# Second half of the projection columns exchanged between two passes: v beside k, retention's q and k beside q

## The chip, the core and the metric

The kernel runs on one core of a Trainium2 chip. The metric is device time in microseconds of one execution, as the median of several. The core's engines run side by side, each through its own queue in order, and meet by semaphores: TensorE (PE) multiplies, VectorE (DVE), ScalarE (ACT) and GpSimd (POOL) work elementwise, SyncE (SP) issues most transfers; ACT and POOL issue some from their own queues.

## The reference, cut

```python
h = rms_norm(x, norm_gain)                    # x: 4096 x 1024
proj = h @ w_in                               # 1024 x 3584
qa, ka, va, ga, qr, kr, vr, gr = split(proj, (512, 512, 512, 512, 256, 256, 512, 512))
# A: 8 heads of 64, rotary positions, three dilated windows, merged by their denominators
attn = dilated_attention(rope(qa), rope(ka), va)
# B: 4 heads, key 64, value 128, decay, in chunks of 128, GroupNorm
ret = group_norm(retention(rotate(qr), rotate(kr), vr)) * ret_gn_gain
mixed = concat([silu(ga) * attn, silu(gr) * ret])
out = rms_norm(x + mixed @ w_out, final_gain)
```

## The kernel before, in words

Three stages follow each other. Stage 1 projects x on q, k, v of the attention (`qa`, `ka`, `va`, here q, k, v) and on retention's `qr` and `kr` (here r), and stores them in DRAM, rotated and split into a high and a low part where attention needs it. Stage 2 runs attention over these and, as filler between its steps, retention in chunks c of 128 tokens, with `vr` projected chunk by chunk (weights `w2`, x chunks `hr`). Stage 3 does gates, output projection and the last norm.

Stage 1 makes two passes over the eight blocks of 512 tokens: blocks q = 0 to 7 are the first pass, 8 to 15 the second, `NBLK` is 8. A pass produces 512 output columns in two banks of PSUM: bank 0 is k in the first pass and q in the second; bank 1 is r in the first and v in the second. The product of a block is formed by seven smaller ones (Strassen and Winograd, `PRODUCTS` = P1 P5 P6 P3 P7 P2 P4) over halves of the columns, of the tokens (`half`) and of the 1024 inputs. Each is done in three matmul passes with high and low parts (`ops` in `product`). A product and a bank make one step, so a block is 14 steps (`STEPS`); block q begins at step s = 14 q. Which engine does what, and at which step, is written out by hand: `at(step, fn, ...)` puts a call into the list of a step; the loop at L773 issues the matmuls of a step and then its calls in the order of registration, which is by block. So each engine's queue follows steps, and within a step the older block comes first.

The calls of one block:

- `load_x` (POOL's queue) brings four quarters of x transposed; `sum_t` (DVE) makes the sums that the products need, `hi_x` (ACT) and `lo_x` (DVE, L316) split a product's input.
- `load_n` brings 128 rows of x into the one buffer `xn`; `square` (ACT, L330) sums their squares. After four of them `root` forms the scale (DVE, POOL: power at L337, `diag` at L339), `along_free` (PE, L348) spreads it along the row and `copy_rb` (ACT) stores it as `rb`. `rb` scales the tables of sines and cosines (`load_table` on POOL's queue, `scale_table` L369 on POOL); `rs` holds the scale by token, for v.
- `snapshot` (ACT, L418 or L416) copies a bank before the next product is added to it, `join` (DVE, L433 or L429) adds a snapshot to another bank. Bank 1 of the second pass is v: its snapshots and joins work on halves and multiply by the token's scale at once; `last_v` (DVE, L532) does the quarter without a snapshot. `store_values` writes v three times, by SP and by POOL.
- `rotate` (DVE, L477 to L482) turns a half of a bank by six instructions; `hi_o`, `lo_o` split q or k, `store_o` and `store_r` write them by SP.

`xn` and `diag` share one buffer (tag `xn`); v, r and the split q and k share four buffers (tag `hl`); seven buffers hold snapshots (tag `m`).

The weights of a pass are split ahead (`split_w`: ACT high, DVE or POOL low), those of the first in `start`, in the first steps; those of the second around step s = 112 (`load_raw`, `scale_b`, `diff_d`, `sum_s1` to `sum_s4`, `split`, `split_p4`), in space that the first pass gives free. Around step 224 `w2` is loaded and split (L83, L84), and the first chunks of x for retention are loaded and split (`split_h_chunk`, L816 to L819).

## Time and profile before

| | us |
|---|---|
| median of 3 runs | 2457.56 |
| lowest and highest | 2450.71, 2457.86 |
| profiled execution | 2460.55 |
| its span | 2458.7 |
| first product of stage 1 begins | 9.06 |
| first product of attention after its longest early wait | 831.01 |

The profile comes from one execution. A page gives busy time by engine, the span in 40 slices, the chain of work that ended last, and groups of instructions by source line; the trace behind it can be asked for any stretch, tile or line. In a row of groups stand line, engine, operation, output and input with their shapes, count, busy time in us and the mean of one in ns, then the idle time of the engine in front of them and what ended it. In a row of waits stand who waited, for whom, total us, times, and the longest. DVE is busy for 1757.4 us of the span, PE for 2306.5.

### The profile page before, as it was taken

What the parts mean: (1) busy time and instruction counts of PE and PEld (TensorE: products, weight loads), DVE (VectorE), ACT (ScalarE), POOL (GpSimd) and SP (SyncE); (2) the same over time, 40 slices, a digit from 0 to 9 for tenths busy, and PEclk for the clock granted to TensorE, in tenths of its full rate; (3) what the DMA queues carried; (4) which work ended last, traced back from release to release, by engine and by line L of the source; (5) the groups of instructions that cost most, each with busy time, mean ns of one, the idle gap of its engine ahead of it and who ended that gap; (6) DMA issues with size and microseconds to landing.
All of it is one profiled execution on the core that took longest, in us unless ns stands there. A gap on an engine that the chain in (4) does not pass through costs nothing.

```text
span 2458.7 us, 47420 instructions
## 1 busy us (share of the span) xinstructions
PE 2306.5 (94%) x16808; PEld 2072.8 (84%) x16808; DVE 1757.4 (71%) x4221; ACT 1115.2 (45%) x3036; POOL 903.1 (37%) x1053
## 2 busy tenths in 40 slices
PE   5798988699998799999999999998899999999998
PEld 5788988699998688888888888886789999999997
DVE  5778977977767587787877788786665565565554
ACT  3444433423333366666666666666322232232221
POOL 2444444344434454353534444446212112121110
PEclk8899999799999899999999999999999999999999
DMA  6454666366667858576585857655676665666663
GB/s 163 146 188 156 198 188 199 110 193 213 196 203 216 215 130 194 135 171 158 135 183 122 203 124 171 163 123 167 173 162 177 146 157 158 146 153 166 143 156 90
DMA packets 457597, 405.07 MB, mean 165 GB/s; under 512 B 207912, under 2 KB 411816, under 8 KB 452240
## 3 DMA queue, kind: packets, MB, share of 16 engines
q1 hardware_dynamic: 422496, 326.62, 52.3%
q0 software_dynamic: 34576, 75.16, 10.5%
q8 instruction: 133, 2.18, 0.4%
q14 instruction: 104, 0.85, 0.1%
q10 hardware_dynamic: 288, 0.26, 0.0%
HBM read 283.12 MB, written 118.64 MB: 163 GB/s over the span
## 4 chain that ended last, share of the span: by engine, by line
PE 68%; DMA 5%; DVE 5%; issue 2%; ACT 1%; SPq 1%; POOL 1%; POOLq 0%; DVEq 0%; ACTq 0%
PE S L1051 8%; PE x L397 7%; PE O L1121 7%; PE T L1088 5%; PE po L48 4%; PE po L50 4%; PE po L49 4%; PE g L50 4%; PE g L49 4%; PE g L48 4%; PE z L397 3%; PE V L48 2%; PE V L50 2%; PE V L49 2%; PE y L397 2%
## 5 line engine op out<-in xcount | busy, mean ns | idle before, releaser
L1072 DVE CUSTOM_DVE_ANT_0 S<-S,mask 128x256 f32<-128x256 f32 (+1 forms) x768 | 308.6, 402 | 165.7 <-PE S L1051 130.4
L1079 ACT ACTIVATE P<-S,nm 128x256 f32<-128x256 f32 (+1 forms) x768 | 337.2, 449 | 47.8 <-DVE nm L1072 44.8
L50 PE MATMUL g<-h,wg 128*128 128x256 f32 x1024 | 289.8, 283 | 0.0
L312 ACT ACTIVATE h<-xt 128x1024 fp32r<-128x1024 f32 (+1 forms) x115 | 119.2, 1037 | 236.1 <-DVE xt L304 107.1
L1635 POOL TENSOR_TENSOR rs<-v,mhalf 128x1 f32<-128x1 f32 x32 | 17.5, 547 | 549.0 <-DVE v L1633 493.5
L1088 PE MATMUL T<-ident,P 128*128 128x128 f32 x1368 | 213.2, 273 | 0.0
L49 PE MATMUL po<-wo,m 128*128 128x512 f32 x512 | 200.4, 391 | 0.0
L316 DVE TENSOR_TENSOR h<-xt,h 128x1024 fp32r<-128x1024 f32 (+1 forms) x115 | 150.8, 1316 | 64.9 <-ACT h L312 63.0
L50 PEld LDWEIGHTS g<-h,wg 128*128 128x128 f32 x1024 | 196.2, 192 | 0.0
L1121 PE MATMUL O<-pt,v 128*64 128x128 f32 (+1 forms) x1968 | 195.6, 325 | 0.0
L1051 PE MATMUL S<-kk,qc 128*128 128x256 f32 x1024 | 187.2, 306 | 7.4 <-issue 2.9
L48 PE MATMUL po<-wohi,m 128*128 128x512 f32 x448 | 178.7, 399 | 6.7 <-ACT m L40 5.6
L1051 PEld LDWEIGHTS S<-kk,qc 128*128 128x128 f32 x1024 | 149.7, 190 | 36.0 <-issue 17.8
L819 POOL TENSOR_TENSOR hc<-hr,hc 128x512 fp32r<-128x512 f32 x64 | 88.0, 1376 | 250.4 <-ACT hc L818 182.3
L50 PE MATMUL po<-wohi,m 128*128 128x512 f32 x448 | 176.7, 395 | 0.2 <-DVE m L41 0.2
L1121 PEld LDWEIGHTS O<-pt,v 128*64 128x64 f32 x1968 | 120.9, 136 | 60.5 <-issue 31.5
L1574 ACT ACTIVATE e<-g 128x256 f32<-128x256 f32 x128 | 48.2, 378 | 256.0 <-PE g L50 241.3
L1088 PEld LDWEIGHTS T<-ident,P 128*128 128x128 f32 x1368 | 163.7, 141 | 0.2 <-ACT wg0hi L87 0.2
L1079 ACT ACTIVATION_READ_ACCUMULATOR P<-S,nm 128x1 f32 x768 | 157.6, 205 | 0.0
L40 ACT ACTIVATE m<-e 128x256 fp32r<-128x256 f32 x128 | 53.1, 417 | 214.0 <-DVE e L1581 129.7
L49 PE MATMUL g<-h,wg1hi 128*128 128x256 f32 x512 | 146.6, 287 | 2.8 <-DVE h L867 2.5
L48 PE MATMUL g<-h,wg1hi 128*128 128x256 f32 x512 | 145.2, 285 | 4.1 <-ACT e L1574 3.4
(275 smaller groups left out, 6640.5 us busy)
## 6 DMA issues: line engine op xcount, KB each, us to landing
hr<-in_xT_dram SPq DMA_DIRECT2D x64, 512.0 KB
q<-dr_q SPq DMA_DIRECT2D x128, 256.0 KB
xt<-in_xT_dram POOLq DMA_DIRECT2D x60, 512.0 KB, 6.5
wb<-dr_w SPq DMA_DIRECT2D x128, 192.0 KB
o<-dr_o SPq DMA_DIRECT2D x192, 128.0 KB
v<-dr_v SPq DMA_DIRECT2D x94, 256.0 KB
xn<-in_x_dram POOLq DMA_DIRECT2D x32, 512.0 KB, 5.1
dr_k<-hl SPq DMA_DIRECT2D x64, 256.0 KB
```

The lines of the kernel that those rows point to most:

```text
L48: nc.tensor.matmul(out, wh, xh, start=first and i == 0, stop=False)
L49: nc.tensor.matmul(out, wh, xl, start=False, stop=False)
L50: nc.tensor.matmul(out, wl, xh, start=False, stop=last and i == n - 1)
L312: nc.scalar.activation(xs[q, prod][:, 0, ks, :], xq[(q, *SOURCE[prod])][:, ks, :], AF.Copy)
L316: (engine or nc.vector).tensor_tensor(h[:, 1, ks, :], src[:, ks, :], f32(h[:, 0, ks, :]), ALU.subtract)
L397: nc.tensor.matmul(o, l, r, start=first and j == 0, stop=last and j == 2, skip_group_check=True)
L819: nc.gpsimd.tensor_tensor(hc[:, :, 1, :], src, hc[:, :, 0, :].bitcast(F32), ALU.subtract)
L1051: nc.tensor.matmul(s[:, j * 256 : (j + 1) * 256], qq[h, t, half][:, off : off + 128] if br == 0 else it["q"][:, t, i, :], rhs, start=(j == ...
L1072: nc.vector.tensor_tensor_reduce(sv, sv, mask[:, it["br"], c0:256], 1.0, BIG, ALU.add, ALU.min, accum_out=nm[:, col : col + 1])
L1079: nc.scalar.activation(it["P", i // 2][:, i % 2, c0:256], sv, AF.Exp, bias=nm[:, col : col + 1], scale=-1.0, accum_out=den[:, col : col + 1])
L1088: nc.tensor.transpose(t[:, j * 128 : (j + 1) * 128], it["P", bank][:, j // 2, j % 2 * 128 : j % 2 * 128 + 128], ident)
L1121: nc.tensor.matmul(o[64 * bank : 64 * bank + 64, c0 : c0 + 128 * m], vt[h, br, idx // 8][:, idx % 8, :], it["pt"][:, a : a + m, :].rearran ...
```

## The change

The columns of bank 1 trade places: v is projected in the first pass, with k, and r in the second, with q. So `values` on ACT scales and copies v into its output tile after plain snapshots and joins, and R tables are loaded, scaled and used in the second pass. `load_n` goes to ACT's queue, the next one right after the square that frees the buffer; squares get new steps, and `along_free` comes two steps after `root` instead of one. All tables are scaled on DVE. At the passage to the second pass the raw weights come in row blocks by `load_w`, and `scale_b` and `sum_s1` one step later. In the last block the R rotation of half 1 and its store come earlier. `w2` is loaded two steps earlier and split three earlier (the first two row blocks; the others likewise), and the high parts of the first chunks, as well as their first two values, are ACT's.

```diff
-            nc.sync.dma_start(dst[:, 0:256].rearrange("k (u c) -> k u c", c=128), pairs_of(rows, 0 if ps else 512, part))
-            if ps == 0:
-                nc.sync.dma_start(dst[:, 256:512].rearrange("k (u c) -> k u c", c=128), pairs_of(rows, 1024, part))
+            halves = [h.rearrange("k (u c) -> k u c", c=128) for h in (dst[:, 0:256], dst[:, 256:512])]
+            nc.sync.dma_start(halves[0], pairs_of(rows, 0 if ps else 512, part))
+            if ps:
+                nc.sync.dma_start(halves[1], pairs_of(rows, 1024, part))
...
-            nc.gpsimd.dma_start(xn[q, i], io["x"][n * 128 : (n + 1) * 128, :])
+            nc.scalar.dma_start(xn[q, i], io["x"][n * 128 : (n + 1) * 128, :])
...
+            if i < 3:
+                load_n(q, i + 1)
...
-            nc.gpsimd.tensor_tensor(tabs[q, n, half], tabs[q, n, half], rb, ALU.mult)
+            nc.vector.tensor_tensor(tabs[q, n, half], tabs[q, n, half], rb, ALU.mult)
...
-                    if q >= NBLK and bank == 1:
+                    if q < NBLK and bank == 1:
...
-        def is_v(q, bank):
-            return q >= NBLK and bank == 1
-
-        def rcol(q, half, u):
-            n = 4 * (q % NBLK) + 2 * half + u
-            return rs[:, n : n + 1]
-
-        def snapshot(q, s, bank, name, half):
-
-            t = M[q, name, bank] = mp.tile([128, 512], F32, tag="m", name="m1")
-            p = banks[q, s, bank]
-            if is_v(q, bank):
+        def snapshot(q, s, bank, name):
+
+            M[q, name, bank] = mp.tile([128, 512], F32, tag="m", name="m1")
+            nc.scalar.activation(M[q, name, bank], banks[q, s, bank], AF.Copy)
+
+        def join(q, s, bank, name):
+
+            t = M[q, name, bank]
+            nc.vector.tensor_tensor(t, banks[q, s, bank], t, ALU.add)
+
+        vfs = {}
+
+        def values(q, half):
+
+            vf = vfs[q, half] = hlp.tile([128, 2, 512], F32, tag="hl", name="vo1")
+            parts = (M.pop((q, "u2", 1)), M.pop((q, "m5", 1))) if half else (M.pop((q, "m1", 1)), banks.pop((q, "x", 1)))
+            for i, p in enumerate(parts):
...
-                    us = slice(256 * u, 256 * u + 256)
-                    nc.scalar.activation(t[:, us], p[:, us], AF.Copy, scale=rcol(q, half, u))
-            else:
-                nc.scalar.activation(t, p, AF.Copy)
-
-        vfs = {}
-
-        def join(q, s, bank, name, half, part):
-
-            t, p = M[q, name, bank], banks[q, s, bank]
-            if is_v(q, bank):
-                vf = value_tile(q, half)
-                for u in range(2):
-                    us = slice(256 * u, 256 * u + 256)
-                    nc.vector.scalar_tensor_tensor(
-                        vf[:, u, 256 * part : 256 * part + 256], p[:, us], rcol(q, half, u), t[:, us], ALU.mult, ALU.add
+                    n = 4 * q + 2 * half + u
+                    nc.scalar.activation(
+                        vf[:, u, 256 * i : 256 * i + 256], p[:, 256 * u : 256 * u + 256], AF.Copy, scale=rs[:, n : n + 1]
...
-            else:
-                nc.vector.tensor_tensor(t, p, t, ALU.add)
-
-        def value_tile(q, half):
-            if (q, half) not in vfs:
-                vfs[q, half] = hlp.tile([128, 2, 512], F32, tag="hl", name="vo1")
-            return vfs[q, half]
...
-        def last_v(q):
-
-            vf, p = value_tile(q, 0), banks[q, "x", 1]
-            for u in range(2):
-                nc.vector.tensor_scalar(vf[:, u, 256:512], p[:, 256 * u : 256 * u + 256], rcol(q, 0, u), None, ALU.mult)
-
...
-                a, d = {1: (-3, 2), 2: (-7, 2), 3: (-10, 2), 4: (-14, 3)}.get(q, (-16, 3))
+                a, n = (-4 - 2 * (q - 1), (2, 4, 7, 9)) if q < 6 else (-14, (2, 5, 7, 10)) if q == 6 else (-15, (2, 5, 8, 11))
+                at(s + a, load_n, q, 0)
...
-                    at(s + a + d * i, load_n, q, i)
-                    at(s + a + d * i + d - 1, square, q, i)
-                e = s + a + 4 * d
-                at(e, root, q)
-                at(e + 1, along_free, q)
-                at(e + 1, copy_rb, q)
+                    at(s + a + n[i], square, q, i)
+                at(s + a + n[3] + 1, root, q)
+                late = a + n[3] + 3
+                at(s + late, along_free, q)
+                at(s + late, copy_rb, q)
...
-                if one or n == "A":
+                if n == "A" or not one:
...
-                    at(s + max(c, {0: 10, 1: 8}.get(q, 0)), scale_table, q, n, half)
+                    at(s + max(c, 10 if q == 0 else late + 1 if one else 0), scale_table, q, n, half)
...
+                at(s + 11, values, q, 1)
+                at(s + 12, store_values, q, 1)
+                at(s + 14, values, q, 0)
+                at(s + 15, store_values, q, 0)
+            else:
+                end = q == NB2 - 1
...
-                at(s + 17, rotate, q, 1, 1)
+                at(s + (11 if end else 17), rotate, q, 1, 1)
...
-                at(s + 18, store_r, q, 1)
-            else:
-                at(s + 11, store_values, q, 1)
-                at(s + 14, last_v, q)
-                at(s + 15, store_values, q, 0)
+                at(s + (14 if end else 18), store_r, q, 1)
...
-            raw[name] = t = ROOM[room](F32)
+            raw[name] = ROOM[room](F32)
...
-                rows = io["w1"][(k0 + k) * 128 : (k0 + k + 1) * 128, :]
-                nc.sync.dma_start(t[k][:, 0:256].rearrange("k (u c) -> k u c", c=128), pairs_of(rows, 0, part))
-            rows = by_blocks(io["w1"])[:, k0 : k0 + 4, 1536 + 256 * part : 1792 + 256 * part]
-            if room in ("wh0", "wh1", "p40"):
-                nc.sync.dma_start(WHOLE[room][:, :, 256:512], rows)
-            else:
-                for j, w in enumerate(WHOLE[room]):
-                    nc.sync.dma_start(w[:, :, 256:512], rows[:, 2 * j : 2 * j + 2])
+                load_w(1, raw[name][k], part, k0 + k)
...
-        at(s - 7, lambda: scale_b(raw["Bb"]))
...
-        at(s - 6, sum_s1)
+        at(s - 6, lambda: scale_b(raw["Bb"]))
+        at(s - 5, sum_s1)
...
-            ahead["hch"] = {0: [split_h_chunk(nc, hcp, raw["hr"], 0, j, nc.vector) for j in range(2)]}
+            ahead["hch"] = {0: [split_h_chunk(nc, hcp, raw["hr"], 0, j) for j in range(2)]}
...
-        at(s - 8, w2_load)
+        at(s - 10, w2_load)
...
-            at(s - 8 + i, w2_some, (2 * i, 2 * i + 1))
+            at(s - (10, 9, 8, 7)[i], w2_some, (2 * i, 2 * i + 1))
+            at(s - 6 + i, w2_split, (2 * i, 2 * i + 1))
...
-        for i in range(4):
-            at(s - 3 + i, w2_split, (2 * i, 2 * i + 1))
...
-        load_n(0, 0)
-        for n, half in (("A", 1), ("A", 0), ("R", 0), ("R", 1)):
-            load_table(0, n, half)
+        for half in (1, 0):
+            load_table(0, "A", half)
...
-        def squares(i):
-            square(0, i)
-            if i < 3:
-                load_n(0, i + 1)
-
...
-            4: lambda: (plus_times(Bb, Ab, 1, Bb, ALU.add), split_w(0, "P3", Bb)),
-            5: lambda: (squares(0), split_w(0, "P7", Aa, 0)),
-            6: lambda: (squares(1), split_w(0, "P2", Ab, 1)),
-            7: lambda: (squares(2), [load_w(0, Bb2[k], 1, 4 + k) for k in range(4)]),
-            8: lambda: squares(3),
-            9: lambda: (root(0), split_w(0, "P4", Bb2, 1)),
+            4: lambda: (load_n(0, 0), plus_times(Bb, Ab, 1, Bb, ALU.add), split_w(0, "P3", Bb)),
+            5: lambda: split_w(0, "P7", Aa, 0),
+            6: lambda: (square(0, 0), split_w(0, "P2", Ab, 1)),
+            7: lambda: ([load_w(0, Bb2[k], 1, 4 + k) for k in range(4)], square(0, 1)),
+            8: lambda: (square(0, 2), split_w(0, "P4", Bb2, 1)),
+            9: lambda: (square(0, 3), root(0)),
...
-                        if c < 2:
-                            nc.vector.tensor_scalar(res[c]["vch"], pv, ahead["rs"][:, c : c + 1], None, ALU.mult)
-                        else:
-                            nc.scalar.activation(res[c]["vch"], pv, AF.Copy, scale=ahead["rs"][:, c : c + 1])
+                        nc.scalar.activation(res[c]["vch"], pv, AF.Copy, scale=ahead["rs"][:, c : c + 1])
...
-                        hch[c].append(split_h_chunk(nc, hcp, hraw.pop(c), c, 1, nc.vector if c < 2 else None))
+                        hch[c].append(split_h_chunk(nc, hcp, hraw.pop(c), c, 1))
...
-                        hch[c + 1] = [split_h_chunk(nc, hcp, hraw[c + 1], c + 1, 0, nc.vector if c < 1 else None)]
+                        hch[c + 1] = [split_h_chunk(nc, hcp, hraw[c + 1], c + 1, 0)]
```

Left out of this diff: the table `WHOLE` of raw tiles, which only `load_raw` used, and the shorter argument lists of `snapshot` and `join`.

More of the change, by code (lines that the diff above doesn't have):

```diff
@@ L175, in phase1 @@
         make_identity(nc, ident)
-        WHOLE = {}
         def whole(p, tag):
             def get(dt):
-                t = WHOLE[tag] = p.tile([128, 4, 512], dt, tag=tag, name=f"w1{tag}")
+                t = p.tile([128, 4, 512], dt, tag=tag, name=f"w1{tag}")
                 return [t[:, k, :] for k in range(4)]
@@ L187, in get @@
             def get(dt):
-                ts = WHOLE["h0"] = [p.tile([128, n, 512], dt, tag=tag, name=f"w1{tag}") for tag in tags]
+                ts = [p.tile([128, n, 512], dt, tag=tag, name=f"w1{tag}") for tag in tags]
                 return [ts[k // n][:, k % n, :] for k in range(4)]
@@ L580, in phase1 @@
             for n, half, a, c in (("A", 1, -1, 3), ("A", 0, 2, 6), ("R", 0, 4, 8), ("R", 1, 6, 10)):
-                if one or n == "A":
+                if n == "A" or not one:
                     if q:
                         at(s + a, load_table, q, n, half)
-                    at(s + max(c, {0: 10, 1: 8}.get(q, 0)), scale_table, q, n, half)
+                    at(s + max(c, 10 if q == 0 else late + 1 if one else 0), scale_table, q, n, half)
             for bank in range(2):
                 if q:
-                    at(s + 1 + 2 * bank, snapshot, q, "x", bank, "m1", 0)
-                    at(s + 5, snapshot, q, "z", bank, "m5", 1)
-                at(s + 6 + bank, snapshot, q, "x", bank, "u2", 1)
-                at(s + 7 + bank, join, q, "z", bank, "u2", 1, 0)
-                at(s + 9 + bank, join, q, "x", bank, "m5", 1, 1)
-                at(s + 11 + bank, join, q, "y", bank, "m1", 0, 0)
+                    at(s + 1 + 2 * bank, snapshot, q, "x", bank, "m1")
+                    at(s + 5, snapshot, q, "z", bank, "m5")
+                at(s + 6 + bank, snapshot, q, "x", bank, "u2")
+                at(s + 7 + bank, join, q, "z", bank, "u2")
+                at(s + 9 + bank, join, q, "x", bank, "m5")
+                at(s + 11 + bank, join, q, "y", bank, "m1")
             at(s + 10, rotate, q, 0, 1)
@@ L738, in phase1 @@
         for bank in range(2):
-            snapshot(0, "x", bank, "m1", 0)
+            snapshot(0, "x", bank, "m1")
         sum_t(0, 1)
@@ L750, in phase1 @@
         for bank in range(2):
-            snapshot(0, "z", bank, "m5", 1)
+            snapshot(0, "z", bank, "m5")
         sum_t(0, 2)
```

## The prediction

> **What bounds the kernel now.** I read the page first (where in the span TensorE, PE, is not full), then a table of stages, then the waits inside the stages that are not full.
>
> ```profile
> span 2458.7 us, 47420 instructions
> PE   5798988699998799999999999998899999999998
> ```
>
> The second line is PE's busy share in 40 slices of 61 us: the holes are in slices 1 to 8 and around 13 and 28. The change touches the first 13 slices (the projection stage) and the beginning of the next stage. So the table is cut there: q0, q1 to q7 (rest of the first pass), q8 (the passage to the second pass), q9 to q15, and the passage to attention. Columns: length, busy time of PE, weight load, DVE, ACT, POOL with counts, granted clock, DMA share, GB/s.
>
> ```profile
> 0.00:90.65 90.65, 58.48 (x338) 53.28 (x339) 53.17 (x68) 39.09 (x61) 26.98 (x33) 0.85 0.57 145
> 90.65:435.68 345.03, 306.91 (x2369) 298.35 (x2367) 279.29 (x329) 140.89 (x194) 156.94 (x159) 0.95 0.59 182
> 435.68:507.74 72.06, 48.91 (x339) 48.13 (x338) 68.14 (x83) 29.13 (x43) 26.50 (x29) 0.81 0.41 124
> 507.74:788.20 280.46, 280.46 (x2354) 280.42 (x2352) 199.64 (x260) 95.54 (x146) 122.95 (x189) 1.00 0.70 213
> 788.20:831.01 42.81, 21.95 (x75) 15.67 (x73) 21.18 (x45) 2.75 (x8) 21.01 (x26) 0.72 0.81 222
> ```
>
> q9 to q15 are seven blocks in 280.46 us, PE busy in all of it: 40.07 us is what a block costs when PE sets the pace, 2.86 us a step. q1 to q7 hold the same number of products and take 345.03 us, 49.3 us a block: 64.5 us too much, of which 38.1 us is PE idle and 26.4 us is matmuls at a lower granted clock (0.95). An idle microsecond thus costs another 0.7 us. q8 takes 32 us too much, and the passage at 788.20 leaves PE idle for 20.9 us. What the change can win lies in these three rows; q9 to q15 can only lose.
>
> What PE waited for, first in q1 to q7, then in q8 (total, times, longest):
>
> ```profile
> PE rb L348 <- POOL diag L339: 14.7, 6, 4.2
> PE x L397 <- ACT m L418: 8.4, 4, 3.2
> PE z L397 <- ACT m L418: 5.0, 1, 5.0
> PE x L397 <- DVE m L433: 4.7, 1, 4.7
> PE x L397 <- DVE h L316: 3.0, 4, 1.2
> PE x L397 <- DVE o L478: 2.3, 1, 2.3
> ...
> PE x L397 <- DVE h L316: 11.9, 2, 8.0
> PE x L397 <- ACT m L418: 6.0, 1, 6.0
> PE x L397 <- DVE o L478: 5.2, 1, 5.2
> ```
>
> Two thirds of the 38.1 us are two things behind the sums of squares: the PE matmul that spreads the root over the row (`along_free`, waits for POOL's `diag`, 14.7 us) and snapshots that ACT makes late (13.4 us). Why ACT is late is in its own waits from q1 to q7:
>
> ```profile
> ACT xn L330 <- DMA xn<-in_x_dram: 98.7, 23, 8.8
> ACT rb L352 <- PE rb L348: 34.1, 7, 6.1
> ACT w1hr L277 <- DMA w1hr<-in_w_dram: 14.6, 1, 14.6
> ```
>
> ACT is busy for only 140.89 us of 345.03, but it stands for 98.7 us in front of squares whose rows are not there, with the snapshots queued behind it.
>
> **The change part by part.**
>
> *Who does what afterwards.* The rotations of retention leave the first pass and come into the second; v goes the other way. Prices, from q1 to q7 (first two rows and POOL's table row) and from q9 to q15 (the rest):
>
> ```profile
> L316 DVE TENSOR_TENSOR h<-xt,h 128x1024 fp32r<-128x1024 f32 x49 | 70.0, 1442 | 22.3 <-ACT h L312 22.2
> L369 POOL TENSOR_TENSOR tab<-tab,rb 128x512 f32<-128x512 f32 x28 | 52.2, 1867 | 0.4
> ...
> L316 DVE TENSOR_TENSOR h<-xt,h 128x1024 fp32r<-128x1024 f32 x48 | 60.9, 1268 | 36.0 <-ACT h L312 34.4
> L480 DVE TENSOR_TENSOR m<-m,tab 128x512 f32<-128x512 f32 x14 | 9.7, 692 | 0.5
> L429 DVE SCALAR_TENSOR_TENSOR vo<-z,rs_all,m 128x256 f32<-128x256 f32 x14 | 6.1, 480 | 15.1 <-PE z L397 15.1
> L416 ACT ACTIVATE m<-x,rs_all 128x256 f32<-128x256 f32 x28 | 11.6, 470 | 0.0
> ...
> 777.72 0.68 DVE L477 TENSOR_TENSOR t<-m,tab 128x512 f32<-128x512 f32 x1
> ...
> 781.46 0.68 DVE L433 TENSOR_TENSOR m<-y,m 128x512 f32<-128x512 f32 x1
> ...
> L454 POOL DMA_DIRECT2D dr_v<-vo x128 | 69.9, 553 | 108.4 <-DVE vo L429 70.3 <-DVE vo L532 38.1
> ```
>
> The last two timeline rows bracket one rotation: six instructions, 3.74 us. DVE in the first pass is busy 279.29/7 = 39.9 us a block, nearly the 40.07 that PE needs. It loses two rotations (7.5) and gains two scaled tables (2 x 0.69, by the broadcast product of L480). It also loses most of the stretching beside POOL's table products: `lo_x` takes 1442 ns here and 1268 where POOL does half as many, 1.2 us over seven. Estimate 39.9 - 7.5 + 1.4 - 1.2 = 32.6 us, 81%. ACT: 20.1 us + 8 value copies at 0.47 + four issues = 25.3 us a block.
>
> In the second pass DVE has 199.64/7 = 28.5 us. It loses eight half instructions of v (six L429, two of `last_v`: 8 x 0.48 = 3.8), gains three joins and four tables (7 x 0.69 = 4.8) and two rotations (7.5), and loses about 1 us of stretching: 36.0 us of 40.07, 90%. POOL is eased in both (16 issues of `dr_v` at 0.553 move forward; four row loads, two R tables and all products leave the first pass). SP's eight stores a block are dr_v for dr_r.
>
> *Squares.* The row load moves from POOL's queue, where it stood behind `load_x` and tables, to ACT right behind the square that frees the buffer.
>
> ```profile
> DMA to landing us min/median/max: 3.5/5.1/9.2
> ...
> L1547 ACTq DMA_DIRECT2D rt<-dr_ret x2: 351/356/362, 1709.8 to 1710.3; - x2
> ```
>
> A row lands 5.1 us after its issue, an issue on ACT's queue costs 0.36 us, and squares now stand two or three steps apart (5.7 or 8.6 us). So a wait of 98.7/23 = 4.3 us should fall to 0 or 1; behind the waiting square stand snapshots and `hi_x`. The matmul of `along_free` comes two steps after `root` instead of one: 2.86 us more against stalls of 14.7/6 = 2.5 us. What is late next: the DMA engines. The second pass is 0.70 x 40.07 = 28 us of DMA a block with v in it; the first takes that mix over and keeps four row loads (2.1 MB, 6.9 us at 213/0.70 = 304 GB/s), so 35 us, some 0.8 of a block (estimate). That is no bound, but rows will land later than 5.1 us at times, and `hi_o` gets its buffer only when v's stores are down. From both sides: if all three sources go, 64.5 us shrinks to nearly 4 (-60); if only DVE's part (10.0 of 38.1 us) goes, -17. I take a block of 43.3 us, nearer to the full effect because every named source is addressed: **-42 us**.
>
> *Start (q0).* The window before 44 us is full of DMA, and one row load and two R tables leave it, but the squares of q0 begin later.
>
> ```profile
> 10.00:44.20 34.20, 19.68 (x95) 17.83 (x95) 16.08 (x19) 13.02 (x21) 6.52 (x5) 0.88 0.99 227
> ...
> 58.81 1.04 ACT L330 ACTIVATE xn<-xn 128x1024 f32<-128x1024 f32 x1
> ...
> 74.62 1.06 ACT L330 ACTIVATE xn<-xn 128x1024 f32<-128x1024 f32 x1 [3.91 <-DMA xn<-in_x_dram]
> ...
> 78.28 1.13 PE L348 MATMUL rb<-diag,ones 128*128 128x512 f32 x2 [1.37 <-POOL diag L339]
> ```
>
> 1 MB at 227 GB/s is 4.6 us earlier for the weights. Four squares ran from 58.81 to 75.7. Now the first comes a step later, each next needs 1.06 + 0.36 + 5.1 = 6.5 us, and P4's split stands between the last two: the last ends near 79 and `along_free` near 81.5 instead of 78.28, with PE waiting 8 to 10 us for it while everything else is some 5 us ahead. Bounds -5 (weights only) and +8 (lost clock too); I take **+4 us**.
>
> *Passage to the second pass (q8).* DVE is busy 68.14 of 72.06 us: DVE sets this stage, with P1 to P4 of new weights to split. Out go q7's two rotations (7.5), in come four tables (2.8). Before it, ACT stood 14.6 us for raw weights behind retention's stores on SP's queue, and those stores are gone from there; the factor (`scale_b`) and the sum behind it come one step later. Against this the raw loads are 32 DMAs instead of 21 and their R half is in 512-byte pieces. DVE then needs some 61 us for 40 of PE, part of it paid out in q7, which ends with slack. Bounds -8 and -28, taken between: **-19 us**.
>
> *Second pass.* DVE's 36.0 us are unevenly laid. I add them up by step, with 0.62 us for a 512 form (3.74/6, the pitch inside the rotation) and 1.15 for a 1024 form (a little under twice, estimated). Steps 10 to 13 and 0 to 2 hold 5.0 (join, rotation, table), 2.9, 0.6, 5.0 (`lo_o`, rotation), 2.3, 4.9 (rotation, sum) and 1.15 us. Against 2.86 us a step, DVE is late by 2.1, 2.2, 0, 2.1, 1.6, 3.6 and 1.9 us after them. Step 3 then has a rotation (3.74), a sum and `lo_x` of P3 (2.3): done 8.0 us after the step's start, where PE needs it at step 6, after 8.6. By step 8 the lag is gone. So the bound is just met; nearest is the row of q9 to q15, which has no idle at all. Bounds 0 and +52 (eight blocks at 46.6 us, a third better than 49.3). I take half a microsecond a block: **+4 us**.
>
> *Passage to attention.* The last v is no longer stored there; the last R rotation of half 1 is drawn forward six steps, the split of w2 three or more, and the first chunks go to ACT.
>
> ```profile
> PE V L48 <- DVE hc L816: 4.8, 1, 4.8
> PE V L49 <- DVE w L84: 2.9, 1, 2.9
> ...
> 809.40 0.58 SPq L447 DMA_DIRECT2D dr_v<-vo  x1
> ...
> 814.01 4.10 SPq L523 DMA_DIRECT2D dr_q<-hl  x4
> ...
> 818.75 0.37 SPq L807 DMA_DIRECT2D hr<-in_xT_dram  x1
> ...
> 829.52 0.63 ACT L818 ACTIVATE hc<-hr 128x512 fp32r<-128x512 f32 x1 [24.83 <-DMA hr<-in_xT_dram]
> ```
>
> The 4.8 and 2.9 us go. `hr` of chunk 2 stands on SP behind four dr_v stores (4.6 us) and the last dr_q; now behind four dr_r and dr_q, released by a DVE that has no w2 splits left. Between -2 (only the wait for hc is saved) and -16 I take half of PE's idle 20.9: **-10 us**.
>
> **Sum:** +4 - 42 - 19 + 4 - 10 = -63 us, against this execution's own 2460.55 us (span 2458.7 and 1.9 around it). The median of the runs is 2457.56, 3 less, so the forecast is 2394 us.
>
> **The skill against the trace.** The row is the 98.7 us of waiting for xn. The Trainium skill, DMA: Bandwidth & Descriptors, "Issuing engines are not separate DMA queues", says that the engine which starts a DMA matters only for the sequencer's own time, since all run on the same 16 engines. By that rule alone the move to ACT's queue saves nothing of the transfer. The trace agrees that the transfer is not what is late (5.1 us against spacings of 5.7): my gain is in the order of issue.
>
> The row for tables on POOL is 1867 ns against DVE's 692. The Trainium skill, Perfetto Trace Analysis, "Optimizing Scalar/DVE Operations", advises the other direction where DVE is saturated, with a warning that the two engines share a read port. By it the second pass would keep four tables off DVE, 33.2 instead of 36.0 us a block, and its +4 in the sum would be 0 (2390 us in all); but `lo_x` at 1442 beside more of POOL's products and 1268 beside fewer shows that POOL's products stretch DVE's, so I keep the +4.
>
> **Rivals.**
> *Rows still late.* The squares' wait stays, because rows queue with v's stores. Then 28.1 us of the idle (diag, snapshots) and 0.7 of it in clock stay, 47.5 of 64.5: -17 instead of -42, 2419 us. For it: DMA at 0.8; against: 5.7 us of room. 18%. This is also what the Trainium skill, DMA: Bandwidth & Descriptors, would leave of the move by that sentence.
> *Everything goes.* First pass at -58, q8 at -27, tail -15, start -1, second pass +4: 2361 us. For it: PE without idle at 71% DVE in q9 to q15. 15%.
> *DVE saturates the second pass.* At 46.6 us a block +52 instead of +4: 2442 us. 7%.
> *The same, slower than before.* `lo_x` of P3 or P6 misses its step in every block and the lower clock doubles it, as in the first pass, where DVE at 81% kept PE waiting. From 48.4 us a block (63 + 4 over eight) the whole gain is gone. At a third of what q8 loses, 10.7 us a block, it is +85: 2475 us. Against it: no xn waits there, and POOL's products are gone. 6%. Another 4% ends between, without a measurable change.
>
> **How the numbers follow.** The forecast has 50% and alone spans 2375 to 2412. With the better case and late rows, 83%, the range is 2360 to 2430. 0.3% (7 us) is what a measurement here can tell. Faster: 50 + 18 + 15 + 7 = 90%; same 4%; slower 6%.
>
> **What would show it.** After: q1 to q7 near 303 us with ACT's wait for xn under 30 us and `along_free` under 5; q8 near 53; q9 to q15 within 286, DVE near 252 busy; first attention products 10 us closer to the end of the products; q0 a few microseconds longer with one wait of 8 us for diag. The forecast is wrong if PE shows waits for `lo_x` in every block of the second pass, or if ACT waits for buffers under v's stores.

## The result, and the profile after

| | before | after |
|---|---|---|
| median, us | 2456.43 (6 runs) | 2441.73 (6 runs) |
| lowest, highest | 2450.46, 2458.25 | 2438.32, 2446.74 |
| ratio after/before | | 0.9946, 95% interval 0.9929 to 0.9963 |
| profiled execution, its span | 2460.55, 2458.7 | 2446.74, 2445.0 |

Faster, but by 14.7 us (0.5%, the interval is clear of 1) and not by 63: 2441.73 lies outside the range 2360 to 2430. The page of the kernel after, PE's busy share in 40 slices of 61 us:

```profile
span 2445.0 us, 47407 instructions
PE   6789997899996899999999999998899999999998
```

The hole in slices 7 and 8 (the end of the first pass and the passage to the second) is shallower than before, that in slices 13 and 14 (the passage to attention) is still there, and slices 2 and 3, in the first pass, are still not full. The same stages of the kernel after (length, busy PE, weight load, DVE, ACT, POOL, granted clock, DMA share, GB/s):

```profile
0.00:89.15 89.15, 57.26 (x339) 51.18 (x339) 56.79 (x77) 44.97 (x70) 22.31 (x30) 0.81 0.56 157
89.15:421.19 332.04, 296.76 (x2369) 290.74 (x2367) 211.81 (x254) 162.02 (x244) 126.83 (x179) 0.95 0.70 219
421.19:482.65 61.46, 46.75 (x338) 45.63 (x337) 57.70 (x72) 29.97 (x44) 30.05 (x38) 0.86 0.57 169
482.65:768.80 286.15, 284.02 (x2354) 283.65 (x2352) 251.31 (x341) 90.76 (x125) 64.91 (x93) 0.99 0.56 170
768.80:818.78 49.98, 22.43 (x73) 16.22 (x73) 24.52 (x46) 5.67 (x14) 13.79 (x16) 0.71 0.70 171
```

| stage | before | after | difference | forecast |
|---|---|---|---|---|
| q0 | 90.65 | 89.15 | -1.5 | +4 |
| q1 to q7 | 345.03 | 332.04 | -13.0 | -42 |
| q8 | 72.06 | 61.46 | -10.6 | -19 |
| q9 to q15 | 280.46 | 286.15 | +5.7 | +4 |
| to the end of attention's early waits | 42.81 | 49.98 | +7.2 | -10 |
| rest | 1627.69 | 1626.22 | -1.5 | 0 |

DVE did what was worked out for it: 211.81/7 = 30.3 us a block in the first pass (32.6 forecast), 251.31 us in the second (252). DMA is at 0.70 in q1 to q7 where it was 0.59, and the clock there is 0.95 as before, with PE still idle for 35.3 us (38.1 before). What PE waited for in q1 to q7 of the kernel after (total, times, longest):

```profile
PE x L398 <- ACT m L406: 22.6, 5, 10.3
PE x L398 <- DVE m L411: 6.4, 1, 6.4
PE z L398 <- ACT m L406: 3.4, 3, 1.6
PE rb L349 <- POOL diag L340: 2.9, 3, 1.8
```

`along_free` fell from 14.7 to 2.9 us, DVE's many small waits are gone, and snapshots rose from 13.4 to 26.0. ACT's waits in the same stretch:

```profile
ACT xn L329 <- DMA xn<-in_x_dram: 73.0, 17, 8.8
ACT w1hr L276 <- DMA w1hr<-in_w_dram: 11.8, 2, 11.5
```

ACT still stands 73.0 us (98.7 before) in front of a square whose row has not landed. One such row, in ACT's timeline:

```profile
97.76 0.33 ACTq L322 DMA_DIRECT2D xn<-in_x_dram  x1
...
109.56 1.06 ACT L329 ACTIVATE xn<-xn 128x1024 f32<-128x1024 f32 x1 [6.80 <-DMA xn<-in_x_dram]
...
111.12 0.60 ACT L406 ACTIVATE m<-x 128x512 f32<-128x512 f32 x1 [0.41 <-ACT xn L329]
```

The row was asked for at 97.76, right behind the square that freed the buffer, and is squared at 109.56: 11.8 us later for a load whose median was 5.1 in the kernel before. The snapshot stands behind it, and PE behind the snapshot for 8.2 us. The stretch in which it was under way:

```profile
97.80:110.00 12.20, 5.77 (x49) 5.56 (x47) 5.65 (x5) 5.06 (x6) 2.56 (x4) 0.87 0.90 272
```

DMA share 0.90 at 272 GB/s: v's stores, which the first pass took over, run at this moment, beside k's stores and loads of tables and x.

### The profile page after: what moved, and what is told of

Read it like the earlier page. It is cut to its first block, busy times and chain, and to the rows that moved or that the text cites. A ratio compares the mean times of both kernels' runs of the same rounds, so it can differ in the third digit from the quotient of the medians.

```text
span 2445.0 us, 47407 instructions
## 1 busy us (share of the span) xinstructions
PE 2298.1 (94%) x16808; PEld 2065.6 (84%) x16808; DVE 1734.5 (71%) x4223; ACT 1141.5 (47%) x3082; POOL 803.8 (33%) x973
## 4 chain that ended last, share of the span: by engine, by line
PE 71%; DMA 11%; DVE 7%; issue 5%; ACT 3%; POOL 2%; SPq 1%; ACTq 0%; DVEq 0%; POOLq 0%
PE S L1019 8%; PE x L398 8%; PE O L1089 7%; PE T L1056 5%; PE po L48 4%; PE po L50 4%; PE po L49 4%; PE g L50 4%; PE g L48 4%; PE g L49 4%; PE z L398 4%; DMA xn<-in_x_dram 3%; PE V L48 3%; PE V L50 2%; PE V L49 2%
## 5 line engine op out<-in xcount | busy, mean ns | idle before, releaser
L315 DVE TENSOR_TENSOR h<-xt,h 128x1024 fp32r<-128x1024 f32 (+1 forms) x115 | 137.5, 1196 | 66.5 <-ACT h L311 66.4
L48 PE MATMUL g<-h,wg0hi 128*128 128x256 f32 x512 | 144.5, 282 | 1.7 <-ACT e L1539 1.7
```

The source lines that it names most:

```text
L48: nc.tensor.matmul(out, wh, xh, start=first and i == 0, stop=False)
L315: (engine or nc.vector).tensor_tensor(h[:, 1, ks, :], src[:, ks, :], f32(h[:, 0, ks, :]), ALU.subtract)
```

## The experiments

All start from the kernel after, unless another is named. Each time is a median with its ratio to the kernel before, run beside it on the same chip. The kernel before took 2456.43 to 2461.86 us there (medians), so the medians of two runs are comparable to some 5 us only, and where that matters the ratio decides. A view shows one execution: q1 to q7 took 332.04 us in the kernel after, and 330.94 and 324.62 in two runs below that change nothing in this stage (first chunks on DVE, q's loads on ACT). A few microseconds in one stage therefore say little.

**Only the squares.** The kernel before, with the change's loads and steps of the squares (row loads on ACT's queue behind the square, new steps, `along_free` two steps after `root`) and nothing else.

> The kernel before, with only the squares' part of the change: rows from ACT's queue behind the square, the new steps, along_free two steps after root; v stays in the second pass, tables on POOL. Theory: without v's stores in the first pass rows land in about 5 us, ACT's wait for xn falls from 98.7 to under 50 us and PE's for diag from 14.7 to under 6; q1 to q7 from 345 to 320 to 330 and the whole to 2432 to 2444, near the whole change's own 2441.7 or under it. Rival (ACT's queue is slow by itself): wait near 73 or over, the whole 2450 or over.

2447.05 us, ratio 0.9947 (0.9927 to 0.9966). In its q1 to q7, 331.9 us long, ACT waited:

```profile
ACT xn L330 <- DMA xn<-in_x_dram: 70.2, 20, 7.4
```

and among PE's waits there were:

```profile
PE x L399 <- DVE m L435: 6.9, 1, 6.9
PE x L399 <- DVE h L316: 6.5, 6, 1.3
...
PE z L399 <- ACT m L420: 3.8, 1, 3.8
```

The whole came a little above the range that was written down, and the wait for rows is well above the 50 expected. This part alone has the whole change's ratio (0.9946), so in the sum nothing can be told apart that the rest, exchange of columns included, brought. It is not that the rest did nothing: q8 is 70.33 us here and 61.46 after the whole change, and the second pass and the passage to attention took that back. The run also shows that rows come late without v's stores in the first pass, where retention's stores stood instead; the bytes beside the row need not be v's. But nearly the same wait of ACT costs differently: PE waited 6.5 us for snapshots here and 19.8 for DVE, and 26.0 and 6.4 after the whole change, where ACT also has v's copies to make (162.02 us busy against 140.54). That these copies are the reason was not tested.

**Row loads back on POOL's queue.**

```diff
-            nc.scalar.dma_start(xn[q, i], io["x"][n * 128 : (n + 1) * 128, :])
+            nc.gpsimd.dma_start(xn[q, i], io["x"][n * 128 : (n + 1) * 128, :])
```

> The changed kernel, with the row loads of the squares (xn) issued from POOL's queue again; steps and all else as changed. Theory (v's stores): rows land late in the first pass because v's three copies fill the DMA engines (share 0.90 at 89 to 110 us of the changed kernel's profile), whatever queue issues them; on POOL they stand besides behind v's own issues, so ACT's wait for xn in q1 to q7 goes from 73 us to 90 or more, q1 to q7 from 332 to 340 to 355 us, the whole to 2450 to 2465. Rival (ACT's queue is the slow one): landing is short again, the wait falls under 40 us and the whole to 2425.

2461.56 us, ratio 1.0012 (0.9996 to 1.0028): no better than before, and some 16 us above the kernel after by the ratios (19.8 by the medians). Its q1 to q7:

```profile
87.53:435.69 348.16, 301.94 (x2368) 296.59 (x2367) 214.46 (x255) 160.13 (x245) 140.33 (x208) 0.92 0.68 210
```

The move to ACT's queue is worth some 16 us in this stage (348.16 against 332.04); ACT's wait for rows is 91.4 us on POOL's queue and 73.0 on its own. This is the part of the row's lateness that the order of issue made, and it came as expected.

**Short rows.** A row load and its square take 16 of 1024 columns, so the sums of squares are of 16 columns and the rest of the row is left out.

```diff
-            nc.scalar.dma_start(xn[q, i], io["x"][n * 128 : (n + 1) * 128, :])
+            nc.scalar.dma_start(xn[q, i][:, 0:16], io["x"][n * 128 : (n + 1) * 128, 0:16])
```

> The changed kernel, but each row load brings 16 of the 1024 columns and the squares sum over these 16 (the scale is another; 98% of the rows' bytes and most of the squares' time left out). Theory: ACT's wait for xn falls from 73 us to under 20, the late snapshots (26 of the 35 us of PE idle in q1 to q7) mostly go, q1 to q7 from 332 to 295 to 305, the whole 2405 to 2418. Rival (snapshots are late because of the value copies and other work on ACT): PE's wait for snapshots keeps above 15 us, the whole above 2428.

2413.16 us, ratio 0.9809 (0.9788 to 0.9829). ACT's wait for rows is 33.1 us, above the 20 expected: even a row of a sixty-fourth of the bytes comes late at times. q1 to q7 are 303.0 us, the figure that the prediction gave for them, but by chance, for the squares are shorter too (ACT busy 139.74 us against 162.02), and the run does not separate this from the row's bytes.

**Two row buffers.** The second buffer shares its space with the R tables, which are not needed in the first pass; each row is asked for one square earlier.

```diff
-            xn[q, i] = tp.tile([128, D], F32, tag="xn", name="xn1")
+            xn[q, i] = tp.tile([128, D], F32, tag="tabR" if i % 2 else "xn", name="xn1")
...
-            if i < 3:
-                load_n(q, i + 1)
+            if i < 2:
+                load_n(q, i + 2)
```

> The changed kernel with a second row buffer (the place of the R tables, idle in the first pass), so that a row is issued one square earlier. Theory: rows of 8 to 13 us of landing are covered by two spacings of 5.7 to 8.6 us; ACT's wait for xn from 73 to 10 to 25 us, q1 to q7 from 332 to 305 to 315, the whole 2412 to 2426. Rival (engines so full that earlier issue only lengthens the landing): wait over 50, the whole over 2435.

2408.65 us, ratio 0.979 (0.9768 to 0.9813). Its q1 to q7, and PE's two longest waits in them:

```profile
85.12:379.79 294.67, 288.29 (x2369) 284.00 (x2367) 211.37 (x253) 161.71 (x245) 122.36 (x178) 0.99 0.77 245
```

```profile
PE x L403 <- DVE m L416: 3.6, 1, 3.6
PE x L403 <- ACT m L411: 2.6, 2, 1.9
```

All bytes are still moved, at a higher DMA share (0.77), and the stage is 37.4 us shorter with the clock at 0.99; ACT's wait for rows is down to 11.2 us. Asking for the row one square earlier is enough to hide its lateness, more so than was expected. It takes 50.4 us off the 345.03 of before, more than the 42 forecast.

**v's third copy written later.** The copies of q1 to q6 are made in the second pass, from the first copy; nothing about the rows is changed. The diff is shortened:

```diff
-                nc.sync.dma_start(dr["v"][2].rearrange("(r q) e -> q r e", q=256)[r0 : r0 + 8], vf[:, u, :])
+                if b in (0, 7): ...                  # as before
+                else:
+                    at(STEPS * (b + 8) + 2 + i, nc.sync.dma_start, third, first_copy)
```

> The changed kernel, in which the third copy of v of the passes q1 to q6 is written in the second pass, from the first copy; nothing of the rows' issue is changed. If the rows come late because v's stores fill the DMA engines, ScalarE's wait for xn falls from 73 to 50 us or less, TensorE's for the snapshots from 26 to under 15, q1 to q7 from 332 to 312 to 322, the kernel to 2422 to 2433. If it is only that the row is asked for too late (a load takes its 4 to 5 us whatever else runs), the wait stays above 65 and the kernel above 2436.

2428.32 us, ratio 0.9865 (0.9846 to 0.9884). Its q1 to q7, and ACT's wait in them:

```profile
89.80:400.46 310.66, 292.55 (x2360) 287.80 (x2359) 213.11 (x252) 161.47 (x244) 124.13 (x178) 0.96 0.68 213
```

```profile
ACT xn L329 <- DMA xn<-in_x_dram: 50.4, 14, 6.2
```

A third of v's stores less, and the wait for rows falls from 73.0 to 50.4, PE's for snapshots from 26.0 to 15.7, the stage by some 20 us (q1 begins at 88.85, one microsecond ahead of the view). The row's issue is as before, so the transfers beside it make a part of its delay.

**First chunks and `vch` on DVE** instead of ACT (an argument in three calls, a `tensor_scalar` for two chunks of `vch`).

> The changed kernel, with the high parts of retention's first chunks and their first two values on DVE again, as before. Theory (the passage to attention is held by DVE's tail of rotations, and by SP's queue, not by who does the first chunks): from the end of the products to the attention products' restart 49.98 us goes to 50 to 54, because the chunk parts then queue behind the same rotations; whole 2441 to 2446. Rival (ACT's part is what made the passage longer than the 42.81 of before): back to 43 to 45, whole 2434 to 2437.

2444.28 us, ratio 0.9946 (0.9927 to 0.9964): no difference, the passage 50.6 us. Who splits the chunks does not set the passage to attention.

**Attention's first q loads on ACT's queue.**

```diff
-            ahead["qq"] = {(0, i, 0): load_q(nc, qp, dr, 0, i, 0) for i in range(2)}
+            ahead["qq"] = {(0, i, 0): load_q(nc, qp, dr, 0, i, 0, nc.scalar.dma_start) for i in range(2)}
```

> The changed kernel, with the first eight loads of q for attention issued from ACT's queue instead of SP's, where they took 785 to 794 us and held dr_r, dr_q and the load of chunk 2 (807.4). Theory: that load is issued near 797, PE's 6.1 us behind it and the 5.1 us for q shrink, the passage from 50 to 40 to 44 us, the whole 2432 to 2437. Rival (the last stores are held by DVE's rotations, or the engines are full): chunk 2 is issued no earlier than 804, the passage above 47.

2433.86 us, ratio 0.9909 (0.9888 to 0.9931): 7.9 us below the kernel after. SP's queue at the passage is this in the kernel after, with what ACT and then PE waited for behind the last of these loads:

```profile
785.39 9.08 SPq L892 DMA_DIRECT2D q<-dr_q  x8
795.48 6.08 SPq L477 DMA_DIRECT2D dr_r<-or  x4
802.06 5.24 SPq L509 DMA_DIRECT2D dr_q<-hl  x4
807.40 0.54 SPq L775 DMA_DIRECT2D hr<-in_xT_dram  x1
...
817.29 0.63 ACT L786 ACTIVATE hc<-hr 128x512 fp32r<-128x512 f32 x1 [30.61 <-DMA hr<-in_xT_dram]
...
818.78 1.22 PE L1019 MATMUL S<-kk,q 128*128 128x256 f32 x4 [6.12 <-ACT P L1047]
```

`hr` of chunk 2 is asked for at 807.40, 38.6 us after the products' end (30.6 before). ACT stands for it until 817.29 with attention's first step (`P`) queued behind, and PE behind that: this load ends the passage. In the run with q's loads elsewhere the products end at 761.37:

```profile
795.73 0.37 SPq L775 DMA_DIRECT2D hr<-in_xT_dram  x1
...
803.16 0.75 PE L1019 MATMUL S<-kk,q 128*128 128x256 f32 x4 [1.98 <-ACT P L1047]
```

The load is asked for 34.4 us after the products' end and ACT goes on 5.95 us later (9.9 in the kernel after), so the passage is 41.8 us. That is as expected and explains the gain. Not all is won, for ACT is now held by issuing q's loads:

```profile
PE V L48 <- ACT vch L1388: 18.9, 1, 18.9
```

**Raw weights Bb on ACT's queue**, since `scale_b` waits 11.8 us for them and they stand last of 24 loads on SP's.

> The changed kernel, with one raw weight (Bb, eight transfers) issued from ACT's queue, so that it no longer stands behind v's stores and the other raw weights on SP's. Theory (q7 and q8 are long because scale_b waits 11.5 us for Bb and DVE stands idle 8.4 us, which it then lacks): the wait falls under 4 us, q7 and q8 together from 110.6 to 100 to 104 us, the whole 2431 to 2436. Rival (DVE's work alone sets q8): q7 and q8 107 to 111, the whole 2438 to 2443.

2453.29 us, ratio 0.9984 (0.997 to 0.9999): worse than the kernel after by 11.6; q7 and q8 together take 117.4 us. ACT's timeline:

```profile
387.09 1.07 ACT L311 ACTIVATE h<-xt 128x1024 fp32r<-128x1024 f32 x1 [1.66 <-issue]
401.70 0.39 ACTq L233 DMA_DIRECT2D w1hr<-in_w_dram  x1
...
408.36 1.08 ACT L406 ACTIVATE m<-z 128x512 f32<-128x512 f32 x2 [20.20 <-DMA w1hc<-in_w_dram]
```

ACT does nothing from 388 to 408 but wait to issue eight loads, though PE was done with their space by 387.0; PE then waits 16.3 us for the snapshot behind them. Why the first issue waited until 401.70 is not settled; SP's own issues took up to 1.9 us each until 398, at a DMA share of 0.95. The expected cure was wrong: a load in a compute engine's queue is cheap only where its issue is not held.

**Tables scaled on POOL**, as before the change.

> The changed kernel, with the tables scaled on POOL again. Theory (lock and slower product: lo_x is stretched beside POOL's products; in the first pass POOL also has v's issues in order, so tables come late and hold the rotations): second pass q9 to q15 286.15 us stays within 3 us, since DVE loses 2.8 us of work a block and gains stretching, first pass + 5 to + 20 us, whole 2446 to 2465. Rival (DVE has too much in the second pass, POOL is free): q9 to q15 282 to 284 and the whole 2434 to 2440.

2446.86 us, ratio 0.9959 (0.9945 to 0.9974): its interval overlaps that of the kernel after, so nothing is told apart in the whole. The first pass was expected to grow and did not (q1 to q7 325.42 us). But q8 grew to 67.6 us, so POOL is no relief for DVE there, though DVE is full.

**Two row buffers and q's loads on ACT**, both edits at once.

> Two row buffers in the first pass and attention's first q loads on ScalarE's queue, both at once. If the late rows and SyncE's full queue at the passage are two separate losses, they add: 2408.7 of the first alone less the 7.9 that the second alone took off the changed kernel, 2399 to 2402 us, with q1 to q7 at 293 to 297 us and the passage to attention near 39. If ScalarE held by issuing q's loads costs what it saves, as the 18.9 us wait for vch suggests it may, 2406 to 2410.

2401.13 us, ratio 0.977 (0.9751 to 0.9788). Two separate losses: 40.6 us below the kernel after, where the two alone made 33.1 and 7.9. The passage to attention is 42.1 us, above the 39 expected. Its q1 to q7 and q8:

```profile
85.58:380.78 295.20, 288.38 (x2368) 283.88 (x2367) 212.04 (x253) 161.83 (x245) 124.47 (x178) 0.99 0.78 245
380.78:442.93 62.15, 47.61 (x338) 46.79 (x337) 57.99 (x71) 29.97 (x44) 30.80 (x39) 0.84 0.55 164
```

q8 stands at 62.15 us, where 53 were forecast. The next five runs ask why.

**P3's low splits at q8 on POOL**, from the kernel with both.

```diff
-        at(s + 1, split, 1, "P3", "S4")
+        at(s + 1, split, 1, "P3", "S4", None, nc.gpsimd)
```

> The kernel with both, and the passage's four low splits of P3 on GpSimd in place of VectorE. If VectorE's 58 busy us of q8's 62 bound q8, four splits of 0.65 us off it give q8 near 59 and 2397 us. If GpSimd makes them slower than VectorE did and P3's products wait for them (its tables made q8 6 us longer when they were put there), q8 stays at 62 or grows to 66: 2400 to 2404 us.

2401.4 us, ratio 0.9764 (0.9748 to 0.9779): no difference. DVE's work in q8 fell to 55.05 us, and q8 is 61.92. PE's first wait in it is for P1's `lo_x` and is 7.5 us (7.7 in the kernel with both); P3's splits stand behind that in DVE's queue, so taking them away can't shorten it.

**Low splits of the second pass as copies on ACT**, from the kernel with two row buffers; the subtraction that makes the low parts is left out.

> The kernel with two row buffers, in which the second pass's low splits of the first weight's products are copies by ScalarE and not VectorE's differences, but for the eight on GpSimd: values differ, and 20 VectorE instructions of some 0.72 us are gone. If VectorE's work bounds q8, it falls from 62.2 to between 50 and 55 us and the kernel to 2397 to 2402. If late raw weights bound it, q8 stays above 59 and the kernel above 2405.

2409.78 us, ratio 0.9796 (0.9781 to 0.9812): not faster than the kernel with two buffers, q8 68.56 us. DVE's waits in q8:

```profile
DVE h L321 <- ACT h L317: 15.0, 3, 7.6
```

DVE, with less to do (50.73 us), waits for ACT instead, which has the copies queued ahead of `hi_x`. The run doesn't separate the two theories: it put the work on the one engine that DVE waits for.

**Bb ahead of Aa on SP**, from the kernel with both, in which DVE waits 7.4 us for `scale_b` before q8.

> The kernel with two row buffers and q's loads on ScalarE's queue, and SyncE asks for the passage's raw weights Bb ahead of Aa, whose eight loads stood before it. If q8 is late because Bb lands late (VectorE sits idle for 6.4 us before q8 for it, and its rotations and sums then push P1's lo_x, for which TensorE waits 7.7 us, to 387.5 us), the wait for lo_x falls under 4 us, q8 from 62.2 to 55 to 58 us and the kernel to 2393 to 2398. If VectorE's own work bounds the passage, the idle time is only moved and q8 stays above 60, the kernel at 2399 to 2403.

2400.83 us, ratio 0.9761 (0.9745 to 0.9777): no gain; q8 is 59.86 us, and q7 49.02 instead of 45.81. DVE's wait moved to the difference that POOL makes from Aa:

```profile
DVE w1wh L268 <- POOL w1q L272: 8.6, 2, 7.0
```

**A store of v behind the raw loads**, from the kernel with both: the four issues that stood on SP ahead of all 24 raw loads go behind them, and the same store's issues on POOL come later with them.

```diff
-                at(s + 15, store_values, q, 0)
+                at(s + (20 if q == NB2 // 2 - 2 else 15), store_values, q, 0)
```

> The kernel with two row buffers and q's loads on ScalarE's queue; pass q6's second half of v is stored behind the passage's 24 raw loads on SyncE, not ahead of them, where its four issues held the queue from 340.0 to 346.9 us. If the late raw weights cost q8 its time, they land some 6 us sooner, VectorE's 6.4 idle us before q8 shrink under 2 and q7 and q8 together lose 4 to 7 us: 2394 to 2398 us. If VectorE's work alone bounds the passage, or the loads wait for their rooms in any case, no change: 2399 to 2403.

2394.47 us, ratio 0.9727 (0.9706 to 0.9748), the lowest of all; the interval lies below that of the kernel with both. Its q1 to q7 and q8:

```profile
84.39:375.71 291.32, 286.84 (x2369) 282.33 (x2367) 213.82 (x254) 162.37 (x245) 126.33 (x179) 1.00 0.78 244
375.71:437.86 62.15, 45.87 (x338) 45.04 (x337) 58.30 (x69) 30.00 (x44) 28.07 (x38) 0.86 0.62 181
```

DVE's wait ahead of q8 is down to 1.6 us. The gain lies in q7, which falls from 45.81 to 40.34 us, nearly what a block without any wait takes; none of it is in q8, where DVE is busy for 58.30 of 62.15 us. PE's waits in q8:

```profile
PE x L403 <- DVE h L315: 7.2, 1, 7.2
PE z L403 <- DVE h L315: 6.4, 1, 6.4
```

and DVE's work ahead of the first of these:

```profile
372.65 1.67 DVE L471 TENSOR_TENSOR m<-m,tab 128x512 f32<-128x512 f32 x1
374.25 1.77 DVE L472 TENSOR_TENSOR o<-o,t 128x512 f32<-128x512 f32 x1
375.94 1.75 DVE L473 TENSOR_TENSOR o<-o,m 128x512 f32<-128x512 f32 x1
377.62 2.42 DVE L268 SCALAR_TENSOR_TENSOR w1hr<-w1q,gain_all,w1hr 128x512 f32<-128x512 f32 x2
379.96 1.40 DVE L268 SCALAR_TENSOR_TENSOR w1hc<-w1q,gain_all,w1hc 128x512 f32<-128x512 f32 x2
381.29 0.68 DVE L416 TENSOR_TENSOR m<-y,m 128x512 f32<-128x512 f32 x1
381.89 1.21 DVE L315 TENSOR_TENSOR h<-xt,h 128x1024 fp32r<-128x1024 f32 x1
```

No gap: `lo_x` at 381.89 comes when the rotation of q7 and the sums ahead of it in the queue are done. Three instructions of the rotation take 1.7 us here instead of 0.68, while POOL splits weights (372.37 to 378.82). So with the loads in time the beginning of q8 waits for what stands in DVE's queue. This is read from the timeline; none of these runs brought q8 near 53 us by easing that queue, and the run with low copies shows ACT's `hi_x` close behind it.

**Both, and the third copy later**, the same without the moved store.

> The same two changes, and the third copy of v of q1 to q6 written in the second pass from the first copy. If late rows were the only thing that the full DMA engines cost the first pass, and two buffers have cured it, q1 to q7 stay at 293 to 296 us and the kernel at 2398 to 2403 (0 to 2 us of it the second pass's added transfers). If the load still costs elsewhere, above all the raw weights ahead of q8, q7 and q8 lose 3 to 7 us: 2394 to 2398.

2394.79 us, ratio 0.9744 (0.9722 to 0.9766), q1 to q7 290.5, q8 62.16. The interval overlaps that of the run before and that of the kernel with both (0.9751 to 0.9788), so a gain is likely but not shown. DVE still waits 6.5 us for the raw weights ahead of q8 (7.4 in the kernel with both), so this is not the cure of the run before.

## Why the prediction was wrong, step by step

**q1 to q7, -42 forecast, -13.0 measured.** The step that failed is "a wait of 98.7/23 = 4.3 us should fall to 0 or 1". It measured 73.0/17 = 4.3 us: the waits became rarer, not shorter. The step set the landing time of the kernel before (median 5.1 us, with DMA at 0.59 in this stage) against spacings of 5.7 or 8.6, and called DMA at 0.8 of a block "no bound". An average over a block hid the bursts: the row that was 11.8 us under way had a share of 0.90 beside it, and a row with one buffer has no slack for that. The runs show it from two sides: with a second buffer the stage fell to 294.67 us, and with a third of v's stores taken away to some 311. v's bytes are only a part of it, since with the squares' part alone ACT waited 70.2 us for rows as well; what the exchange added is that the wait reached PE through the snapshots (26.0 us against 6.5).

The rival "rows still late" described this and priced the stage well (-17), but had 18%. It named v's stores alone as the reason. The Trainium skill, DMA: Bandwidth & Descriptors, "Issuing engines are not separate DMA queues", on which that rival drew, says that initiating a DMA from another engine saves only the sequencer's time. For the transfer the trace agrees, and the prediction's "the transfer is not what is late" did not hold: 22.6 us of the wait for rows went with a third of v's stores. The order of issue within a queue, of which that section says nothing, was worth some 16 us of this stage (348.16 against 332.04). With two buffers the stage fell by 50.4, so the other steps of this term (DVE's work, `along_free`, the clock that comes back with the idle time) were right, and a little too careful.

**q8, -19 forecast, -10.6 measured.** "DVE then needs some 61 us for 40 of PE, part of it paid out in q7" was right in its first half, with DVE busy for 57.70 us inside q8, and failed in its second: some 8 us of this would have had to move into q7, and nothing did. q7 of the kernel after, and that of the kernel with v's store behind the raw loads:

```profile
372.04:421.19 49.15, 42.77 (x339) 42.33 (x337) 29.51 (x35) 22.40 (x35) 22.65 (x30) 0.93 0.81 230
...
335.37:375.71 40.34, 40.34 (x339) 40.10 (x337) 30.54 (x34) 22.39 (x35) 23.35 (x30) 1.00 0.93 251
```

DVE has the slack in q7 (29.51 of 49.15 us busy), but the work that fills q8 does not come early enough to use it. Late raw weights, for which DVE stood 8.6 us in q7, cost q7 and not q8: with the loads in time q7 is 40.34 us, DVE still busy for only 30.54 of it, and q8 still 62.15. An order of steps that draws q8's splits into q7 was not tried, so the cause of q8's length stays open beyond the reading of DVE's queue above.

**Passage to attention, -10 forecast, +7.2 measured.** The waits for DVE's `hc` and `w` went as forecast. The step that failed is the reading of SP's queue: the stores of r were set equal to those of v, and q's eight loads, which stand in the same queue ahead of `hr`, were not counted at all. They took 9.08 us of issue (6.88 before) and r's last stores 6.08, and `hr` was asked for 8 us later after the products' end than before. The term has the wrong sign, and the bounds of -2 and -16 excluded a loss without a reason. With q's loads on another queue the passage was 41.8 us: 8.2 of the 17 us are explained by that, the others stay open.

**Second pass, +4 forecast, +5.7 measured**: the size is right, and DVE's load too (251.31 us busy, 252 forecast), but the reason is not. Half a microsecond a block was forecast for uneven DVE work, and PE has no wait at all in q9 to q14. A block without any wait is 40.31 us here, from the start of q9 to that of q10 in PE's timeline, and 40.07 before, which was not foreseen and makes 1.7 us over seven blocks. The rest is in the last block, which takes 44.3 us with one wait of 2.1 us for a join and slower matmuls behind it (clock 0.96). That the sum agrees is partly luck.

```profile
482.65 5.92 PE L398 MATMUL x<-h,w1kk 128*128 128x256 f32 x48
522.96 5.92 PE L398 MATMUL x<-h,w1kk 128*128 128x256 f32 x48
```

**q0, +4 forecast, -1.5 measured**: the wait for `diag` is there, just under the 8 to 10 us forecast, but `along_free` ran at 74.45 us where 81.5 was worked out, and the rest of q0 became shorter by more than the wait; inside the bounds.

```profile
74.45 2.07 PE L349 MATMUL rb<-diag,ones 128*128 128x512 f32 x2 [7.55 <-POOL diag L340]
```

Sum: of the 49 us that are missing, 29 are in q1 to q7, 17 in the passage to attention, 8 in q8 and 2 in the second pass; q0 gave 5.5 back and the rest 1.5. They have no single cause. In the first, one row buffer stood against bursts of transfers, which the runs show. In the second, loads and stores stood in one queue ahead of the load that ends the passage, which one run shows for half of it. In q8 it is the order of DVE's work, which is only read from the timeline. The first two have in common that queues and DMA engines were counted on average, or not at all.

## What to carry to other kernels

When work moves from one stage to another, move its transfers on paper too: for each load on the path, list what stands ahead of it in its queue and what runs on the DMA engines at that moment, not in the mean of a block. What a late load costs depends on what stands behind it: nearly the same wait of ACT for rows cost PE 6.5 us of snapshots in one kernel and 26.0 in another. A load into a single buffer that is asked for when the buffer comes free has only the time between two uses; a second buffer, here in space that another stage owns, was worth 33 of the 47 us between the kernel after and the best one. A load moved to a compute engine's queue gains where it is out of order in the old one, and loses where its issue can be held up.

## What the runs showed of the hardware

ACT's issue of eight loads into space that had been free since 387.0 us began at 401.70 and held the engine's compute work for 20.2 us, while SP was issuing 16 loads; SP's own issues, 0.37 us when quiet, took up to 1.9 us in that stretch, at a DMA share of 0.95. DVE's rotation instructions of 0.68 us took 1.67 to 1.77 us beside POOL's splits of weights (store of v behind the raw loads). And the products of r cost 0.24 us a block more than those of v (40.31 and 40.07 us), with no wait in either; v's rows name the weights first among what they read (`x<-w1kk,h`), r's name x's split first (`x<-h,w1kk`); why the difference costs time is open.
